# Turning the first FFN's normalised tiles by plain transposes, starting the fifth down product's weight sums in the first, and pairing two late modulation vectors

## The chip, the core and the metric

The kernel runs on one core of one Trainium2 chip. The metric is device time in microseconds (us) of one execution, start to end, on that core. Engines are named as the profile names them: PE is TensorE's matmul stream and PEld its weight loads, DVE is VectorE, ACT is ScalarE, POOL is GpSimd, SP is SyncE. SP starts most of the loads from DRAM (queue q1), POOL starts the accumulating ones (queue q0), ACT a few small ones.

## The reference, cut to what matters

Two layers of a hybrid backbone work on 512 latent and 256 context tokens with D = 1024. Layer 0 has a mixer of gated linear attention and softmax attention, layer 1 a recurrent mixer (HGRN2); after each comes a SwiGLU FFN with 2816 hidden columns. Every sub-layer is wrapped in norms and modulated by vectors m that are computed from the conditioning vector c. Only the latent stream is returned.

```python
def _rms(x, gain): return x * rsqrt(mean(x * x) + 1e-6) * gain
def _modulate(h, shift, scale): return h * (1 + scale) + shift
def _swiglu(h, w_gate, w_up, w_down): return (silu(h @ w_gate) * (h @ w_up)) @ w_down

for l in range(2):
    m = split(silu(c) @ mod_w[l] + mod_b[l], 6)         # for latent tokens; the same with c_ctx for context
    h = _modulate(_rms(x, norm_pre_mix[l]), m[0], m[1])
    o = mixer_l(h)
    x = x + m[2] * _rms(o @ w_out, norm_post_mix[l])
    h = _modulate(_rms(x, norm_pre_ffn[l]), m[3], m[4])
    x = x + m[5] * _rms(_swiglu(h, ...), norm_post_ffn[l])
```

## The kernel before, in words

All data is float32. A matmul of full precision is made of three in the faster fp32r type: each operand is split into a high part H (an ACT cast of the value) and a low part L (DVE: the value less H), and `mm3` adds H·H, H·L and L·H in PSUM. So each weight tile that comes from DRAM as `raw` costs one ACT cast (`wH`) and one DVE subtraction (`wL`) before PE can use it.

Tokens stand in six tiles of 128 (four latent, two context), and the hidden dimension in blocks of 128. A tile has its tokens in the partitions. A matmul wants the hidden dimension there, so a normalised tile has to be turned in eight blocks of 128x128; `h` holds the turned H and L parts.

In order of time, by the profiled execution: the even mixer and its out-projection (to about 420 us), the first FFN's gate and up matrices (about 430 to 749), its down matrix (749 to 911), the odd mixer's first product (to 986) and the rest of that mixer with its out-projection (to about 1345), the second FFN (its down matrix from about 1562 to 1667) and the end.

**The FFN's body.** Gate and up are computed by a Strassen-like scheme of seven products for two halves of the tokens and of the columns, for eleven pairs of column blocks. Between the products `fill` (L1595) takes a step of a generator called `extra`, which is `mod_late` (L560) in the first FFN: it computes the modulation vectors that are needed later. One job of `mod_late` loads the 1024x1024 blocks of `mod_w` in eight row strips, multiplies each by the conditioning value of its rows and adds it to an accumulator `macc` on DVE (L597 and the line of the first strip), one operation for each strip and vector. When all strips are in, eight matmuls with a vector of ones (`mod_acc<-macc,one`) sum the partitions, the sums are turned on PE into columns, and a copy puts them where they are used. `macc` has room for two vectors, and PE's eight matmuls are the same whether one or two of them are in use. `per` says how many DVE operations make a step. A job whose last entry is a tuple also makes gate rows in DRAM (`gate_rows`): one more small turn and a store. The code's steps that are left are taken at the ninth of the eleven pairs (L1665). This part isn't pinned: a planner may shift instructions within an engine's order.

**The down matrix (`down`, L1690).** It is cut into quarters B(k, j), rows k and columns j, and computed by seven products named 11, S1, N3, SN, S3, 22 and 12, each over eleven row blocks in six groups: one block, then five times two. `operands` (L1728) makes a product's weights and factors for one group, two or three groups ahead of PE. It is pinned: the order of the code is kept. Weights come from three places:
- 11, N3 and 12 load a quarter as `raw` on SP's queue.
- S1, SN and 22 use t, a sum that grows: in product 11, t3 is loaded with B(0,1) and DVE writes t = B(0,0) + t3; in S1, POOL's accumulating load adds B(1,1) to t; in SN it adds B(1,0).
- S3 uses t3 + B(1,1): B(0,1) is there since product 11, and POOL's accumulating load adds B(1,1) in product N3 (L1768).

The sums of product 11's first three groups are owed: they are run after `finish()` of the body, the others at once.

**The first FFN's end.** In product 12 each finished tile goes through `post_norm` (the gated residual `xr`), then `pre_norm` (L679): ACT's square with a row sum, a power on POOL (`rs`, L668), which is the factor 1/rms of each token. Here two ways part. At the mixers' ends (`forms`), DVE scales the tile by rs (`xn`, L695) and PE turns xn by transposes with the identity (L358). At the first FFN's end DVE scales the 128x128 identity instead (`dg`, L689), and a matmul of the tile by dg turns and scales in one. `pair_turn` (L715) does this for two tiles at a time: four groups of four 128x128 blocks into one PSUM tile, then for each group two ACT operations that modulate into `hf`, ACT's cast to H and DVE's subtraction to L (L734, L735). The groups are taken one by one between the token tiles of the odd mixer's first product (`nat`), by `turn_step`. From the start of product 12 to the last turned group, `order_from` and `order_to` tie the instructions of ACT and DVE to the order of the code.

Of the kernel before, what the change touches and what calls it, by code (L numbers as in the profile page):

```python
# [8 lines left out]
F32 = mybir.dt.float32  # L9
# [4 lines left out]
ALU = mybir.AluOpType  # L14
# [3 lines left out]
P = 128  # L18
D = 1024
# [11 lines left out]
R_C, R_CC, R_NPM, R_MB, R_NQM, R_NPF, R_NQF, R_BG, R_LB, R_GG, R_HG, R_END = 0, 8, 16, 32, 128, 144, 160, 176, 180, 212, 213, 214  # L31
# [285 lines left out]
class Net:  # L317
# [358 lines left out]
        self.squared = self.nc.scalar.activation(junk, src, AF.Square, accum_out=ss)  # L676
        return ss

    def pre_norm(self, pool, t, xt, A, B, h):  # L679

        nc = self.nc
        r = 0 if t < LT else 1
        forms = isinstance(h, Forms)
        xn = pool.tile([P, D], F32, tag="xn", bufs=2, name=f"xn{t}") if forms else None
        rs = self.rstd(self.sumsq(xt, xn), D)
        yield
        if not forms:
            dg = pool.tile([P, P], F32, tag="dg", bufs=4, name=f"dg{t}")
            self.mark = nc.vector.tensor_scalar(dg, self.ident, rs, None, op0=ALU.mult)  # L689
            self.pair.append((xt, dg))  # L690
            if len(self.pair) == 2:
                self.turns.append(self.pair_turn(pool, t - 1, self.pair, A, B, h))
                self.pair = []
            return
        self.mark = nc.vector.tensor_scalar(xn, xt, rs, None, op0=ALU.mult)  # L695

        def turn():
            for hf in range(2):
                pt = self.tr_tile(f"hT{t}{hf}")
                f = h.at(hf, t)  # L700
                for kk in range(4):
                    k = hf * 4 + kk
                    self.tr(pt[:, kk * P : (kk + 1) * P], xn[:, k * P : (k + 1) * P], self.ident)
                for kk in range(4):
                    k = hf * 4 + kk
                    src = pt[:, kk * P : (kk + 1) * P]
                    nc.scalar.activation(f[:, kk, :], src, AF.Identity, bias=B[:, r, k : k + 1], scale=A[:, r, k : k + 1])
                h.put(hf, t)

        self.turns.append(turn)  # L710

    def pair_turn(self, pool, t, pair, A, B, h):

        nc = self.nc
        r = 0 if t < LT else 1  # L715
        tok = slice(t * P, t * P + 2 * P)

        for q in range(4):
            pt = self.tr_tile(f"hT{t}{q}").rearrange("p (k i) -> p k i", k=2)
            f = pool.tile([P, 2, 2 * P], F32, tag="hf", bufs=2, name=f"hf{t}{q}")  # L720
            for kk in range(2):
                k = 2 * q + kk
                for a, (xt, dg) in enumerate(pair):
                    self.mm(pt[:, kk, a * P : (a + 1) * P], xt[:, k * P : (k + 1) * P], dg, start=True, stop=True)
            for kk in range(2):
                k = 2 * q + kk
                nc.scalar.activation(f[:, kk, :], pt[:, kk, :], AF.Identity, bias=B[:, r, k : k + 1], scale=A[:, r, k : k + 1])
            self.latest = self.put(h, slice(2 * q, 2 * q + 2), tok, f)
            if q < 3:
                yield  # L730
# [777 lines left out]
    def post_pre(self, pp, y, t, gvs, xsrc, xdst, nxt, cuts):  # L1508

        nc = self.nc  # L1510
        xt = pp.tile([P, D], F32, tag="xt", bufs=2 if nxt and isinstance(nxt[2], Forms) else 4, name=f"xr{t}")
        nc.sync.dma_start(out=xt, in_=xsrc(t))

        def store(c):
            nc.sync.dma_start(out=xdst(t)[:, c], in_=xt[:, c])

        yield from self.post_norm(y, xt, gvs[0 if t < LT else 1], cuts, xdst and store)
        if nxt is not None:
            A, B, h = nxt
            yield from self.pre_norm(pp, t, xt, A, B, h)  # L1520

    def turn(self, left=0):

# [182 lines left out]
    def down(self, l, fp, qp, rp, xp, quad, early, tiles, n, ending, finish):  # L1706


        nc = self.nc
        np_, nh = NFC // 2, n // P  # L1710
        B = lambda k, j, i: self.blocks[k][:, i, 512 * j : 512 * j + 512]
        groups = [slice(0, 1)] + [slice(i, i + 2) for i in range(1, 11, 2)]
        ng = len(groups)
        v = nc.vector
# [5 lines left out]
        t, t3 = (lambda i: part(1, i)), (lambda i: part(0, i))  # L1720
        spare = []
        turns = [0, 0]
        add = lambda o, src: self.pin(nc.gpsimd.dma_start(out=o, in_=src, accum_op=ALU.add))  # L1723
        load = lambda o, src: nc.sync.dma_start(out=o, in_=src)
        seven = (("11", "X"), ("S1", "O"), ("N3", "Q"), ("SN", "X"), ("S3", "X"), ("22", "O"), ("12", "X"))
        owed = []

        def operands(p, g):  # L1728
            i = groups[g]
            m = i.stop - i.start  # L1730
            name = seven[p][0]
# [12 lines left out]
            a = [x[:, :m] for x in rings[turns[1] % 3]]  # L1744
            turns[1] += 1
            if name in ("N3", "S3"):
                f = spare[0][:, turns[0] % 2, :m]
                turns[0] += 1
                if name == "N3":
                    v.tensor_tensor(f, quad(0, 0, i), quad(0, 1, i), op=ALU.add)  # L1750
                else:
                    v.scalar_tensor_tensor(f, quad(1, 1, i), -1.0, quad(0, 0, i), op0=ALU.mult, op1=ALU.subtract)
            else:
                f = quad(*{"11": (0, 0), "S1": (1, 0), "SN": (0, 0), "22": (1, 1), "12": (0, 1)}[name], i)
            nc.scalar.copy(H, src)
            nc.scalar.copy(a[0], f)
            v.tensor_tensor(L, src, H.bitcast(F32), op=ALU.subtract)  # L1757
            v.tensor_tensor(a[1], f, a[0].bitcast(F32), op=ALU.subtract)
            if name == "11":
                owed.append(lambda: v.tensor_tensor(t(i), src, t3(i), op=ALU.add))  # L1760
                if g > 2:
                    owed.pop()()
            elif name == "S1":
                x = quad(0, 0, i)
                v.tensor_tensor(x, f, x, op=ALU.subtract)
                add(t(i), B(1, 1, i))
            elif name == "N3":
                add(t3(i), B(1, 1, i))  # L1768
            elif name == "SN":
                add(t(i), B(1, 0, i))  # L1770
            return a, (H, L)
# [12 lines left out]
        dp, y = yield  # L1784
# [81 lines left out]
    def run(self):  # L1866
        nc, I, out = self.nc, self.I, self.out
# [17 lines left out]
        h = Split(ha)  # L1885
        with self.pool("pre0") as pp:
            xT = pp.tile([P, KD, NT], F32, name="xT")
            for t in order:
                xt = pp.tile([P, D], F32, tag="xt", bufs=6, name=f"xt{t}")
                nc.sync.dma_start(out=xt, in_=xin(t))  # L1890
                rs = self.rstd(self.sumsq(xt), D)
                nc.vector.tensor_scalar(xt, xt, rs, None, op0=ALU.mult)
                for hf in range(2):
                    pt = self.tr_tile(f"xT{t}{hf}")
                    for kk in range(4):
                        k = hf * 4 + kk
# [6 lines left out]
            A = self.cst.tile([P, 2, 8], F32, name="aff01")  # L1903
            B = self.mod_m(0, 0)
# [17 lines left out]
            def sums(qd, ks):  # L1922
                if ks[0] == 0:
                    accs[qd] = (self.sc_tile("mod_acc", qd) if qd < 2 else self.tr_tile("mod_acc"))[:, :P]
                for k in ks:
                    for j in range(4):
                        self.mm(
                            accs[qd][32 * j : 32 * j + 32, :],
                            self.scT[:, k, :],
                            us[qd, k // 2 * 2][:, k % 2, j // 2, (j % 2) * P : (j % 2) * P + P],  # L1930
                            start=(k == 0),
                            stop=(k == KD - 1),
                            tile_position=(0, 32 * j),
                        )
                if ks[-1] == KD - 1:
                    accs[qd] = self.mod_cols(0, accs[qd], P, [(m, r, 2 * qd, 2 * m, r, 2) for m in range(2) for r in range(2)])
# [89 lines left out]
        fp = self.open_pool("f0", "right")  # L2026
        mods = self.mod_late(fp, ((1, ((0, 0), (0, 1)), None),), tag="raw", bufs=3)
        forms, pp, rp = project(0, order, yp, I["even_w_out"][0], cat, xin, mods)
        for _ in mods:
            pass  # L2030
        h1 = Split(ha)
        late = self.mod_late(
            fp, ((0, ((5, 0), (5, 1)), (5, R_NQF)), (1, ((1, 0), (1, 1)), None), (1, ((5, 0),), (5, R_NQF, 1)), (1, ((4, 0),), None)),
            per=lambda n: 2 if n > 1 else 3,
        )

        def ending(dp):
# [66 lines left out]
        fp = self.open_pool("f1", "right")  # L2104
# [98 lines left out]
```

## Time and profile before

| | us |
|---|---|
| median of three runs | 1684.37 |
| the three runs | 1682.98, 1684.37, 1687.10 |
| the profiled execution | 1683.48 |
| its span in the trace | 1681.5 |
| PE busy | 1644.6 |
| PEld busy | 1481.0 |
| DVE busy | 1309.8 |
| ACT busy | 917.5 |
| POOL busy | 121.4 |

Times of instructions are counted from the start of the profiled span. The profile has one line for an instruction or a group of them: engine, source line, operation, the output tile and its inputs by name, partitions x elements and type, and the count. "[0.44 <-POOL rs L668]" says that the engine was idle for 0.44 us before it, and that this idle time ended when POOL had written rs. Groups show shortest/mean/longest ns of one instruction and the stretch in which they lie. L355 is the line of the helper through which all matmuls go, L358 that of all transposes, so such instructions are told apart by their tiles.

### The profile page before, as it was taken

Reading aid. Unit: us, or ns where it says so; the run is one execution under the profiler, and the core shown is the slowest. Engines: PE = TensorE matmul, PEld = TensorE weight load, DVE = VectorE, ACT = ScalarE, POOL = GpSimd, SP = SyncE. Lnnn points to the kernel's source line nnn. Section 1 sums busy time; section 2 is a strip of 40 time slices with the busy share of each in tenths; the row PEclk is TensorE's granted clock in tenths of the full one; section 3 lists DMA queues with packets and bytes.
Section 4 is the critical chain, followed back from the end, with each engine's and each line's share of the span. In section 5 each row is a group of like instructions: output and inputs, shape, how many; then the busy total and the mean of one; then the engine's idle time right before and its main releaser. Section 6 shows DMA issues by size and latency. Waiting matters only on the chain.

```text
span 1681.5 us, 32537 instructions
## 1 busy us (share of the span) xinstructions
PE 1644.6 (98%) x13407; PEld 1481.0 (88%) x13407; DVE 1309.8 (78%) x2105; ACT 917.5 (55%) x1560; POOL 121.4 (7%) x129
## 2 busy tenths in 40 slices
PE   6999998999999999999999999999999999999998
PEld 5899997888999999998888888888888899999876
DVE  4889768876898988877668548788775599987887
ACT  4745567836543443445447436666664565555654
POOL 1004110001000000003102000000000100000220
PEclk9999999999999999999999999999999999999999
DMA  9651002164243444348725542121124334333793
GB/s 330 192 155 41 2 27 101 51 207 152 84 147 101 144 143 148 117 150 167 142 73 203 190 129 59 51 64 39 52 64 150 125 111 117 113 101 101 183 206 138
DMA packets 184736, 204.79 MB, mean 122 GB/s; under 512 B 7142, under 2 KB 141836, under 8 KB 184588
## 3 DMA queue, kind: packets, MB, share of 16 engines
q1 hardware_dynamic: 173632, 181.82, 34.3%
q0 software_dynamic: 9024, 17.30, 5.9%
q10 hardware_dynamic: 1932, 3.59, 0.7%
q8 instruction: 105, 1.72, 0.4%
q14 instruction: 43, 0.35, 0.1%
HBM read 193.23 MB, written 9.46 MB: 121 GB/s over the span
## 4 chain that ended last, share of the span: by engine, by line
PE 85%; DVE 7%; ACT 3%; DMA 3%; issue 1%; POOL 0%; ACTq 0%; DVEq 0%; POOLq 0%
PE nat L355 13%; PE a L355 12%; PE ff L355 8%; PE E L355 8%; PE x L355 7%; PE oproj L355 6%; PE o L355 4%; PE D L355 4%; PE b L355 4%; PE fq L355 3%; PE gqk L355 2%; PE pearly L355 2%; PE S L355 2%; PE poh L355 1%; PE attO L355 1%
## 5 line engine op out<-in xcount | busy, mean ns | idle before, releaser
L355 PE MATMUL nat<-wH,x 128*128 128x256 f32 (+2 forms) x968 | 225.5, 321 | 3.0 <-ACT x L734 2.6
L355 PEld LDWEIGHTS nat<-wH,x 128*128 128x128 f32 x968 | 162.2, 190 | 19.2 <-ACT x L734 3.7
L824 ACT CAST wH<-raw 128x1024 fp32r<-128x1024 f32 x120 | 125.0, 1050 | 95.5 <-DVE raw L849 31.4
L825 DVE TENSOR_TENSOR wL<-raw,wH 128x1024 fp32r<-128x1024 f32 x120 | 145.6, 1220 | 21.3 <-ACT wH L824 20.9
L355 PE MATMUL nat<-wL,x 128*128 128x256 f32 (+2 forms) x484 | 153.4, 317 | 0.3 <-DVE wL L770 0.3
L770 DVE TENSOR_TENSOR wL<-raw,wH 128x1024 fp32r<-128x1024 f32 (+1 forms) x83 | 98.7, 1198 | 48.0 <-ACT wH L769 47.1
L355 PE MATMUL ff<-x,wH 128*128 128x512 f32 (+1 forms) x512 | 127.7, 340 | 0.0
L769 ACT CAST wH<-raw 128x1024 fp32r<-128x1024 f32 (+1 forms) x83 | 84.9, 1034 | 68.0 <-PE ff L355 19.9
L668 POOL TENSOR_TENSOR rs<-ms,neghalf 128x1 f32<-128x1 f32 (+2 forms) x62 | 63.5, 1029 | 783.0 <-DVE ms L666 782.9
L355 PE MATMUL oproj<-wH,x 128*128 128x512 f32 x320 | 102.1, 396 | 0.4 <-ACT x L1290 0.4
L355 PEld LDWEIGHTS nat<-wL,x 128*128 128x128 f32 x484 | 92.1, 190 | 6.0 <-DVE wL L770 0.7
L597 DVE SCALAR_TENSOR_TENSOR macc<-mraw,scT,macc 128x1024 f32<-128x1024 f32 x70 | 88.1, 1280 | 10.9 <-DMA mraw<-in_mod_w_dram 10.7
L355 PEld LDWEIGHTS ff<-x,wH 128*128 128x128 f32 x512 | 87.2, 190 | 10.1
L355 PE MATMUL x<-wH,two 128*128 128x512 f32 x280 | 90.5, 392 | 0.9 <-DVE y L1798 0.7
L976 ACT COPY qkh<-arr 128x512 f32<-128x512 f32 x112 | 70.2, 643 | 36.3 <-DVE arr L981 32.1
L1723 POOL DMA_DIRECT2D t<-in_ffn_w_down_dram x36 | 41.8, 1228 | 648.1 <-DVE wL L1757 613.5
L355 PE MATMUL ff<-x,wL 128*128 128x256 f32 (+1 forms) x256 | 86.2, 337 | 0.0
L849 DVE TENSOR_TENSOR raw<-raw 128x512 f32<-128x512 f32 x120 | 82.7, 690 | 2.8
L981 DVE TENSOR_TENSOR arr<-arr,f 128x512 f32<-128x512 f32 x112 | 74.2, 687 | 1.9 <-ACT qkh L976 0.3
L355 PE MATMUL E<-x,wH 128*128 128x384 f32 (+1 forms) x320 | 70.9, 311 | 0.0
L355 PEld LDWEIGHTS oproj<-wH,x 128*128 128x128 f32 x320 | 59.5, 188 | 12.6 <-ACT x L1290 0.9
L355 PE MATMUL b<-x,wH 128*128 128x384 f32 (+1 forms) x320 | 70.5, 309 | 0.0
(420 smaller groups left out, 4540.7 us busy)
## 6 DMA issues: line engine op xcount, KB each, us to landing
mraw<-in_mod_w_dram SPq DMA_DIRECT2D x80, 512.0 KB, 4.4
raw<-in_ffn_w_gate_dram SPq DMA_DIRECT2D x44, 512.0 KB, 4.6
raw<-in_ffn_w_up_dram SPq DMA_DIRECT2D x44, 512.0 KB, 4.3
raw<-in_odd_w_in_dram SPq DMA_DIRECT2D x40, 512.0 KB, 3.8
t<-in_ffn_w_down_dram POOLq DMA_DIRECT2D x30, 512.0 KB, 8.0
raw<-in_ffn_w_down_dram SPq DMA_DIRECT2D x28, 512.0 KB, 7.4
mraw<-in_mod_w_dram SPq DMA_DIRECT2D x32, 256.0 KB, 6.3
raw<-in_even_w_in_dram SPq DMA_DIRECT2D x16, 512.0 KB, 3.8
```

Of the source, the lines that this page charges most:

```text
L355: return self.pin(self.nc.tensor.matmul(*a, **k))
L597: nc.vector.scalar_tensor_tensor(a, u, w, a, op0=ALU.mult, op1=ALU.add)
L668: nc.gpsimd.tensor_tensor(rs, ms, self.neghalf.to_broadcast([P, w]), op=ALU.pow)
L769: nc.scalar.copy(H[:, :m], raw[:, :m])
L770: nc.vector.tensor_tensor(L[:, :m], raw[:, :m], H[:, :m].bitcast(F32), op=ALU.subtract)
L824: self.nc.scalar.copy(H, f)
L825: self.nc.vector.tensor_tensor(L, f, H.bitcast(F32), op=ALU.subtract)
L849: add = lambda o, x, y: nc.vector.tensor_tensor(o, x, y, op=ALU.add)
L976: nc.scalar.copy(qkv[:, :, :, half, :], dst)
L981: nc.vector.tensor_tensor(dst, dst, tb, op=ALU.mult)
L1723: add = lambda o, src: self.pin(nc.gpsimd.dma_start(out=o, in_=src, accum_op=ALU.add))
```

## The change

Three edits, independent of each other.

The first makes the first FFN's end like the mixers' ends: DVE scales the whole tile into xn, which takes the place of the tile y (no longer read then), and PE turns it by transposes with the identity.

```diff
-    def pre_norm(self, pool, t, xt, A, B, h):
+    def pre_norm(self, pool, t, xt, A, B, h, xn):
...
-            dg = pool.tile([P, P], F32, tag="dg", bufs=4, name=f"dg{t}")
-            self.mark = nc.vector.tensor_scalar(dg, self.ident, rs, None, op0=ALU.mult)
-            self.pair.append((xt, dg))
+            self.mark = nc.vector.tensor_scalar(xn, xt, rs, None, op0=ALU.mult)
+            self.pair.append(xn)
...
-                for a, (xt, dg) in enumerate(pair):
-                    self.mm(pt[:, kk, a * P : (a + 1) * P], xt[:, k * P : (k + 1) * P], dg, start=True, stop=True)
+                for a, xn in enumerate(pair):
+                    self.tr(pt[:, kk, a * P : (a + 1) * P], xn[:, k * P : (k + 1) * P], self.ident)
...
-            yield from self.pre_norm(pp, t, xt, A, B, h)
+            yield from self.pre_norm(pp, t, xt, A, B, h, y)
```

The second moves the accumulating loads of t3, in both FFNs, from the third product to the first, each right behind its group's sum t.

```diff
             if name == "11":
-                owed.append(lambda: v.tensor_tensor(t(i), src, t3(i), op=ALU.add))
+
+                def sums():
+                    v.tensor_tensor(t(i), src, t3(i), op=ALU.add)
+                    add(t3(i), B(1, 1, i))
+
+                owed.append(sums)
                 if g > 2:
                     owed.pop()()
...
-            elif name == "N3":
-                add(t3(i), B(1, 1, i))
```

The third makes the last two jobs of `mod_late` in the first FFN, of one vector each (the second layer's 5 and 4), one job of two. The gate rows then come after the pair, and a step is always two DVE operations.

```diff
-            fp, ((0, ((5, 0), (5, 1)), (5, R_NQF)), (1, ((1, 0), (1, 1)), None), (1, ((5, 0),), (5, R_NQF, 1)), (1, ((4, 0),), None)),
-            per=lambda n: 2 if n > 1 else 3,
+            fp, ((0, ((5, 0), (5, 1)), (5, R_NQF)), (1, ((1, 0), (1, 1)), None), (1, ((4, 0), (5, 0)), (5, R_NQF, 1))),
+            per=lambda n: 2,
```

More of the change, by code (lines that the diff above doesn't have):

```diff
@@ L683, in pre_norm @@
         forms = isinstance(h, Forms)
-        xn = pool.tile([P, D], F32, tag="xn", bufs=2, name=f"xn{t}") if forms else None
-        rs = self.rstd(self.sumsq(xt, xn), D)
+        if forms:
+            xn = pool.tile([P, D], F32, tag="xn", bufs=2, name=f"xn{t}")
+        rs = self.rstd(self.sumsq(xt, xn if forms else None), D)
         yield
         if not forms:
-            dg = pool.tile([P, P], F32, tag="dg", bufs=4, name=f"dg{t}")
-            self.mark = nc.vector.tensor_scalar(dg, self.ident, rs, None, op0=ALU.mult)
-            self.pair.append((xt, dg))
+            self.mark = nc.vector.tensor_scalar(xn, xt, rs, None, op0=ALU.mult)
+            self.pair.append(xn)
             if len(self.pair) == 2:
```

## Prediction

> **What bounds the kernel now.** I read the page first, then the list of waits, then the timeline of each stage that the change touches.
>
> ```profile
> span 1681.5 us, 32537 instructions
> PE 1644.6 (98%) x13407; PEld 1481.0 (88%) x13407; DVE 1309.8 (78%) x2105; ACT 917.5 (55%) x1560; POOL 121.4 (7%) x129
> ```
>
> TensorE (PE) is busy 98% of the span, so an instruction less on PE is worth its issue time, unless PE then waits for another engine. That has to be read stage by stage. The windows give the body of the first FFN and its end: us, then busy us (and records) of PE, its weight loads, DVE, ACT and POOL, granted clock, DMA share, GB/s.
>
> ```profile
> 430.00:740.00 310.00, 310.00 (x1804) 305.34 (x1802) 270.09 (x346) 137.29 (x198) 0.00 (x0) 1.00 0.39 118
> 895.00:945.00 50.00, 49.21 (x264) 41.93 (x263) 30.78 (x48) 36.41 (x64) 6.65 (x11) 1.00 0.43 147
> ```
>
> In the body PE has no idle time at all (310.00 of 310.00). In the end it is idle for 0.8 us of 50, and ACT is busy for 36 of 50 where the body has 137 of 310: there ACT and DVE may be close behind PE. That decides the first part.
>
> **The change part by part: the tiles' turning.** Today DVE scales the identity (dg) and a matmul by dg turns and scales at once; then DVE scales the whole tile (xn) and PE only transposes. The parts have rows: dg and its products here, xn and its transposes from the mixers' ends, which are made that way already.
>
> ```profile
> L355 PE MATMUL hT<-dg,xr x96: 270/275/377, 901.7 to 941.2; 128*128 128x128 f32 x96
> L689 DVE TENSOR_SCALAR dg<-ident,rs x6: 278/284/289, 895.5 to 929.2; 128x128 f32<-128x128 f32 x6
> L358 PE MATMUL hT<-ident,xn x80: 270/273/330, 378.3 to 1345.7; 128*128 128x128 f32 x80
> L695 DVE TENSOR_SCALAR xn<-xr,rs x10: 743/754/755, 372.0 to 1342.8; 128x1024 f32<-128x1024 f32 x10
> 904.76 1.05 PE L355 MATMUL hT<-dg,xr 128*128 128x128 f32 x8
> 905.57 0.48 PE L355 MATMUL x<-wH,two 128*128 128x512 f32 x1
> ...
> 381.14 0.66 PE L358 MATMUL hT<-ident,xn 128*128 128x128 f32 x4
> 381.55 0.70 PE L355 MATMUL oproj<-wH,x 128*128 128x512 f32 x2
> ```
>
> Six tiles of eight blocks are 48 products but 96 records: a product with dg runs as two instructions. Ten xn tiles are 80 transposes and 80 records. A group of four products holds PE for 905.57 - 904.76 = 0.81 us, four transposes for 381.55 - 381.14 = 0.41. Twelve groups save 12 x 0.40 = 4.8 us of PE, the bound if nothing else is late. DVE pays 0.754 - 0.284 = 0.47 us more for each of six tiles.
>
> Between the seventh product's start and the last turned tile ACT and DVE keep the order of the code (order_from, order_to), so the delays can be carried down the rows.
>
> ```profile
> 902.27 0.28 DVE L689 TENSOR_SCALAR dg<-ident,rs 128x128 f32<-128x128 f32 x1
> 903.23 1.06 ACT L676 ACTIVATE junk<-y 128x1024 bf16<-128x1024 f32 x1 [2.14 <-DVE y L1798]
> ...
> 916.36 0.50 PE L355 MATMUL nat<-wL,x 128*128 128x512 f32 x1 [0.31 <-DVE wL L770]
> ...
> 918.83 0.29 DVE L689 TENSOR_SCALAR dg<-ident,rs 128x128 f32<-128x128 f32 x1 [0.67 <-POOL rs L668]
> 920.66 1.06 ACT L676 ACTIVATE junk<-xr 128x1024 bf16<-128x1024 f32 x1 [1.80 <-DVE xr L755]
> 930.13 0.69 DVE L735 TENSOR_TENSOR x<-hf,x 128x512 fp32r<-128x512 f32 x1 [0.68 <-ACT x L734]
> ...
> 936.42 0.69 DVE L735 TENSOR_TENSOR x<-hf,x 128x512 fp32r<-128x512 f32 x1 [5.59 <-ACT x L734]
> ```
>
> First pair: two scalings stand ahead of the DVE sum y that starts ACT at 903.23, and ACT's next idle time begins only at 920.66 - 1.80 = 918.86. So ACT starts 2 x 0.47 = 0.94 us later. The third scaling adds 0.47, of which short waits of DVE swallow about 0.36, and the wL for which PE waits at 916.36 already (0.31) comes 1.05 later; so the 1.6 us that its first four groups saved are waited away: PE stands at +1.05 at 916.36. Second pair: the scaling at 918.83 lies just ahead of its group, so PE stands at +1.4; four groups bring back 1.6, but the second group after waits about 0.2 for its PSUM buffer, which ACT frees. The last half tile at 930.13 comes 1.2 later; its end, 930.82, lies some half microsecond ahead of its use, so PE is pushed back to +0.7. Third pair: DVE waits 5.59 us there, nothing is close, and 1.6 come off. **Sum: -0.9 us** of the 4.8; the other bound, with no gain from the transposes at all and the delays kept, is +1.4.
>
> What could make it less is POOL's power for the next tile, which runs beside DVE.
>
> ```profile
> 907.33 0.55 POOL L668 TENSOR_TENSOR rs<-ms,neghalf 128x1 f32<-128x1 f32 x1 [5.78 <-DVE ms L666]
> 910.08 1.39 POOL L668 TENSOR_TENSOR rs<-ms,neghalf 128x1 f32<-128x1 f32 x1 [2.21 <-DVE ms L666]
> 909.85 1.22 DVE L770 TENSOR_TENSOR wL<-raw,wH 128x1024 fp32r<-128x1024 f32 x1
> ```
>
> The same power takes 0.55 us alone and 1.39 beside a wide DVE operation. Two powers follow right on a scaling that grows longer (918.83 and 922.73); if both are stretched by 0.84, up to 1.7 us are lost. I take nothing, since the powers start before the scaling, and keep it for the range. The Trainium skill (SBUF — State Buffer, "SBUF: two separate sides") says that VectorE and GpSimd share a port pair as an exclusive lock, which a VectorE operation in a two-port mode holds for its whole length. The two POOL rows agree; by that rule the part would give +0.8 in place of -0.9.
>
> **The pair of late vectors.** Two jobs of one vector become one job of two.
>
> ```profile
> 685.48 0.34 PE L355 MATMUL D<-x,wL 128*128 128x384 f32 x1
> 685.75 1.06 PE L355 MATMUL mod_acc<-macc,one 128*32 128x512 f32 x8
> 686.75 0.62 PE L355 MATMUL E<-x,wH 128*128 128x384 f32 x2
> ```
>
> A job's end is one group of eight ones-records and four transposes of the summed rows. A record of the body holds PE for 310.00 / 1804 = 0.17 us, so D's last ends its hold at 685.65 and the ones-records hold PE until 686.75: 1.1 us. Four transposes hold it for 0.41 by the row at 381.14. One such end goes: **-1.5 us**, whole, because PE has no idle time here. The sixteen weight loads and multiply-adds stay; eleven steps stay eleven (two vectors' sums in eight steps instead of twice three, one end instead of two). The drain at the ninth pair now holds a gate row instead of a column; its transpose is only moved. Bounds: -1.7, if the record behind each group is late as well, and 0, if PE turns out to wait instead.
>
> **The fifth product's sums.** POOL's six accumulating loads of t3 leave the third product and follow the sums of the first, in both FFNs. POOL's queue keeps its order, so they stand ahead of the second product's loads of t. The question is who else uses DMA then. Here are packets and MB, first of the SP queue (q1) alone at 749 to 757, then of POOL's (q0) and SP's together at 1598 to 1606; then what ACT and PE wait for.
>
> ```profile
> q1 hardware_dynamic: 1335, 2.57, 92.9%
> ...
> q0 software_dynamic: 541, 1.03, 69.8%
> q1 hardware_dynamic: 537, 1.02, 38.8%
> ...
> 753.97 1.06 ACT L1755 CAST wH<-raw 128x1024 fp32r<-128x1024 f32 x1 [1.38 <-DMA raw<-in_ffn_w_down_dram]
> 764.48 0.62 PE L355 MATMUL x<-wH,two 128*128 128x512 f32 x2
> 1602.00 1.05 ACT L1755 CAST wH<-raw 128x1024 fp32r<-128x1024 f32 x1 [4.01 <-DMA raw<-in_ffn_w_down_dram]
> ...
> PEld q L355 <- ACT aH L1756: 0.6, 1, 0.6
> PEld q L355 <- DVE wL L1757: 0.6, 1, 0.6
> ```
>
> Alone, SP's loads run at 0.32 MB a us; beside POOL's they share packet for packet and run at 0.13. In the first FFN the first product's last three raw loads are still to come when t3's first sums are ready (from about 751), and ACT waits for them even now (753.97). At the shared rate I put their arrivals at 757, 761 and 763 instead of 754, 755 and 757. The tightest use is the fifth group's low part at 764.48, for which raw at 761, its cast of 1.06 and DVE's two subtractions (1.22 for the weight's, by the wL row above, and about as much for the factor's) end at 764.5. So I take **+0.3 us**, bounds 0 and +2.5. In the second FFN the raws of the first product are there long before; the third product's late loads (ACT's 4.01 us wait) meet POOL's queue as before, since the second product's sums, moved back by t3's, now fill it until about 1606. So no gain there either; the bounds are PE's two longest waits in that product, the last two rows (from the list of waits between 1556 and 1670): -1.2 if they go, and as much again, +1.2, if one more sum stands ahead of those loads. POOL's issues hide behind PE; t3 is wanted only two products after its old place.
>
> **Sum:** -0.9 - 1.5 + 0.3 = -2.1 us. The profiled execution took 1683.5 us (span 1681.5 and 2.0 around it), so **1681.4 us**; that execution lies 0.9 under the median of before, 1684.4.
>
> **The rivals.** *All PE time arrives.* If ACT and DVE have more slack than the rows say, the turning gives 4.8: 1683.5 - 4.8 - 1.5 = 1677.2 us. For it: PE is idle there for 0.8 us in all. Against it: ACT's 15.6 us without idle time, and the wait at 916.36. *POOL's loads go first.* If the first products' loads must stand behind all queued sums instead of sharing, the third raw load of the first FFN arrives near 760 and costs PE 2.5 us; the third product of the second FFN loses 1.2 more. With the stretched powers (1.7) that is -2.1 + 2.5 - 0.3 + 1.2 + 1.7 = +3.0: 1686.5 us, slower. It decides from the point where the fourth group's raw lands after about 758.5. Against it: 541 and 537 packets side by side. *The turning stays two-pass or the planner reorders the unpinned stretches* so that the pair's end is not saved: about 1683.5, no change.
>
> **How the numbers follow.** Forecast 0.50, all PE time 0.22, loads behind sums 0.18, no change 0.10. The range 1677.0 to 1687.0 reaches to the first rival's time and to the slower one's. A measurement of this kernel tells about 0.3%, 5 us, from no change. Faster than that are most of the first rival (0.18) and the forecast where the second FFN's stall goes too (0.04): 0.22. Slower than that is only the slower rival with its stalls in both FFNs at more than my price: 0.10. The rest, 0.68, is within.
>
> **What would show it.** hT must fall from 96 records to 48 in the end, its groups from 0.81 to 0.4 us; PE's waits for DVE or ACT between 903 and 932 must grow to about 3 us. If they do not, the first step is wrong. The ones-records must fall by eight with no new idle time in the body. In the first FFN's first product ACT must wait longer for raw, and PE little or not; a PE wait there of 2 us says the slower rival. In the second FFN the third product's wait for raw must stay near 4 us; if it goes, its stall of some 1.2 us is gain that I left out.

## The result, and the profile after

The changed kernel takes 1681.69 us (median of 20 runs, 1680.08 to 1683.9) where the kernel before takes 1684.32 (20 runs, 1682.5 to 1687.1): 2.6 us less, a ratio of 0.9985 with a 95% interval of 0.9979 to 0.9991. The forecast was 1681.4. The sum was right, but two of its terms were not, and by luck they cancelled.

The profiled execution took 1680.08 us. The head of its page, and the windows of the first FFN's body and of its end with the same columns as before:

```profile
span 1678.3 us, 32400 instructions
PE 1638.8 (98%) x13347; PEld 1474.3 (88%) x13347; DVE 1312.2 (78%) x2104; ACT 916.9 (55%) x1560; POOL 122.6 (7%) x129
```

```profile
430.00:740.00 310.00, 309.34 (x1794) 305.15 (x1793) 269.48 (x345) 137.01 (x198) 0.00 (x0) 1.00 0.40 118
895.00:945.00 50.00, 46.31 (x219) 35.80 (x218) 34.19 (x49) 36.35 (x64) 7.89 (x11) 1.00 0.44 147
```

PE is busy for 1644.6 - 1638.8 = 5.8 us less, but the span is shorter by 3.2 only: more than two microseconds of the time saved on PE came back as idle time. The windows say where. At the first FFN's end PE is now idle for 3.7 us of 50 (0.8 before), and in the body, where it never stood still, for 0.66.

To place the gains, the start of the same matmul is compared in the two traces. A shift is the start after less the start before; where it changes, time went or came.

| matmul that starts, in the trace of before, at | shift, us | what lies between it and the row above |
|---|---|---|
| 600, first FFN's body | +0.48 | the start of the run; no edit lies here |
| 700, first FFN's body | 0.00 | the pair of late vectors: -0.48 |
| 891, before the last tiles of the down matrix | +0.04 | t3's sums in the first FFN: 0 |
| 916.36, the nat that waits for wL | +1.07 | first pair of tiles: +1.03 |
| 922, behind the second pair's first group | +0.70 | |
| 931.6, after the second pair | +1.02 | second pair: about 0 |
| 941.2, after the third pair | -0.69 | third pair: -1.71 |
| 1371, second FFN's start | -0.39 | no edit lies here |
| 1412, second FFN's body | -1.45 | no edit lies here |
| 1604, third product of its down matrix | -1.47 | |
| 1610, fourth product | -3.07 | t3's sums in the second FFN, if anything: -1.60 |

The first FFN's end, by the list of PE's waits from 895 to 945 in the changed kernel, and the rows of its timeline in which these waits end:

```profile
PE nat L355 <- DVE wL L770: 1.8, 2, 1.3
PE hT L358 <- DVE y L689: 1.6, 2, 1.2
PE hT L358 <- ACT hf L727: 0.2, 1, 0.2
```

```profile
903.57 0.55 PE L358 MATMUL hT<-ident,y 128*128 128x128 f32 x3 [1.21 <-DVE y L689]
914.50 0.50 PE L355 MATMUL nat<-wL,x 128*128 128x512 f32 x1 [0.56 <-DVE wL L770]
917.44 0.50 PE L355 MATMUL nat<-wL,x 128*128 128x512 f32 x1 [1.27 <-DVE wL L770]
920.72 0.55 PE L358 MATMUL hT<-ident,y 128*128 128x128 f32 x3 [0.37 <-DVE y L689]
```

The nat at 917.44 is the one that started at 916.36 before. hT has 48 records of one pass where it had 96, and PE pays for it with 3.6 us of waits for the scaled tile and for the wL that stands behind the scalings on DVE.

The body's new idle time is one place. PE first, then DVE, from the changed kernel's timeline:

```profile
676.39 0.59 PE L355 MATMUL E<-T,wH 128*128 128x384 f32 x2 [0.20 <-DVE go L902]
677.43 0.44 PE L355 MATMUL E<-T,wL 128*128 128x384 f32 x1 [0.46 <-DVE wL L825]
```

```profile
669.76 1.28 DVE L597 SCALAR_TENSOR_TENSOR macc<-mraw,scT,macc 128x1024 f32<-128x1024 f32 x1
672.44 1.29 DVE L597 SCALAR_TENSOR_TENSOR macc<-mraw,scT,macc 128x1024 f32<-128x1024 f32 x1 [1.39 <-DMA mraw<-in_mod_w_dram]
673.64 2.13 DVE L849 TENSOR_TENSOR raw<-raw 128x512 f32<-128x512 f32 x3
675.70 0.55 DVE L902 TENSOR_TENSOR go<-go,E 128x384 f32<-128x384 f32 x1
676.16 1.22 DVE L825 TENSOR_TENSOR wL<-raw,wH 128x1024 fp32r<-128x1024 f32 x1
```

Read from below: PE waits for go and wL; DVE makes them late because it stood still for 1.39 us at 672.44, for a load of mod_w that the second vector of the pair needs in the same step. The two waits are 0.66 us in the rows; -0.48 is left of the 1.5 us that one group of sums less should save, so with what they stretch around them they cost about 1.0 us.

The first product of the first FFN, whose loads now share DMA with t3's sums (the changed kernel's timeline of ACT):

```profile
754.68 1.05 ACT L1755 CAST wH<-raw 128x1024 fp32r<-128x1024 f32 x1 [2.09 <-DMA raw<-in_ffn_w_down_dram]
758.45 1.05 ACT L1755 CAST wH<-raw 128x1024 fp32r<-128x1024 f32 x1 [2.71 <-DMA raw<-in_ffn_w_down_dram]
762.49 1.05 ACT L1755 CAST wH<-raw 128x1024 fp32r<-128x1024 f32 x1 [2.26 <-DMA raw<-in_ffn_w_down_dram]
```

ACT waits longer there, as forecast, and PE doesn't notice: the shift stays at 0.04.

In the second FFN the third product's stall is gone. DMA by queue from 1602 to 1610 (packets, MB, time as a share of 16 engines), in the kernel before and then in the changed one:

```profile
q0 software_dynamic: 543, 1.05, 70.5%
q1 hardware_dynamic: 545, 1.04, 39.2%
```

```profile
q1 hardware_dynamic: 904, 1.72, 57.8%
q0 software_dynamic: 292, 0.53, 39.3%
```

POOL's queue (q0) moves half as much there, and SP's loads (q1) two thirds more. That is not yet why the stall is gone: the load on which it hangs had landed by then, as the last experiment shows.

### The profile page after: what moved, and what is told of

Same layout as the page of the kernel before. It is cut to its first block, busy times and chain, and to the rows that moved or that the text cites. A ratio compares the mean times of both kernels' runs of the same rounds, so it can differ in the third digit from the quotient of the medians.

```text
span 1678.3 us, 32400 instructions
## 1 busy us (share of the span) xinstructions
PE 1638.8 (98%) x13347; PEld 1474.3 (88%) x13347; DVE 1312.2 (78%) x2104; ACT 916.9 (55%) x1560; POOL 122.6 (7%) x129
## 4 chain that ended last, share of the span: by engine, by line
PE 84%; DVE 7%; ACT 4%; DMA 2%; issue 2%; POOL 1%; DVEq 0%; ACTq 0%; POOLq 0%
PE nat L355 12%; PE a L355 11%; PE ff L355 8%; PE E L355 8%; PE x L355 6%; PE oproj L355 6%; PE o L355 4%; PE b L355 4%; PE D L355 4%; PE pearly L355 3%; PE fq L355 3%; PE gqk L355 2%; PE q L355 2%; PE S L355 2%; PE poh L355 1%
```

## The experiments

All times are medians, of 11 runs (20 for the changed kernel); the ratio is to runs of the kernel before on the same chip. The shifts are read from the profiles as above, as changes over a stage: the body (600 to 700; 500 to 700 in the two spaced kernels), the first FFN's end (891 to 941), the second FFN's start (1371 to 1412), its third product (1604 to 1610). The stall of that product is 1.6 us long in the first profile of the kernel before, so -1.60 in the last column says that it is gone, and 0 that it is all there.

| kernel | us | ratio and interval | body | FFN's end | second FFN's start | third product |
|---|---|---|---|---|---|---|
| changed | 1681.69 | 0.9985 [0.9979, 0.9991] | -0.48 | -0.73 | -1.06 | -1.60 |
| before_again | 1683.97 | 0.9997 [0.9988, 1.0005] | +0.37 | +0.01 | -0.15 | -0.11 |
| turn_only | 1683.50 | 0.9996 [0.9987, 1.0005] | +0.23 | -0.74 | -0.08 | -1.59 |
| sums_only | 1682.90 | 0.9992 [0.9984, 1.0001] | +0.01 | 0.00 | +0.69 | -1.59 |
| pair_only | 1684.51 | 1.0002 [0.9994, 1.0011] | +0.30 | 0.00 | +2.59 | -0.07 |
| third_pair | 1681.34 | 0.9985 [0.9976, 0.9994] | -0.16 | -1.77 | +0.06 | -1.59 |
| short_tr | 1682.03 | 0.9992 [0.9983, 1.0000] | +0.50 | -2.14 | -0.79 | -1.16 |
| long_mm | 1684.42 | 1.0005 [0.9996, 1.0014] | +0.02 | +1.50 | -0.38 | -0.72 |
| pair_oneload | 1681.60 | 0.9987 [0.9979, 0.9996] | -1.65 | 0.00 | +0.02 | -1.60 |
| pair_second | 1682.98 | 1.0000 [0.9991, 1.0009] | -0.20 | +0.01 | -0.68 | -1.59 |
| pair_spaced | 1684.13 | 0.9997 [0.9988, 1.0006] | -0.12 | +0.04 | -0.09 | -1.60 |
| third_spaced | 1681.34 | 0.9984 [0.9976, 0.9993] | -0.10 | -1.50 | +0.40 | -1.59 |
| sums_later | 1685.99 | 1.0011 [1.0002, 1.0019] | +0.66 | +0.04 | -0.35 | -1.60 |

What an edit leaves alone shows how much the run itself moves. The first FFN's end moves by no more than 0.04 where the first edit is absent, so 0.1 us can be read there. The body without the third edit lies between 0.00 and +0.66 against the first profile. The second FFN's start moves between -1.06 and +2.59, whatever the edit. In pair_only, where it moves by +2.59, the granted clock is 0.89 from 1371 to 1386, where every other profile has 1.00; so at least a part of that figure is the clock's.

### The kernel before once more

No edit.

> The kernel before once more, for what the run alone moves: the start (up to 1.9 us between the profiles so far), the second FFN's start between 1370 and 1412 (from 1.1 us earlier to 2.6 later), the stall of 1605 to 1609 (there or not). If the stall is there again: it belongs to the place of t3's sums. If not: it comes by the run in the kernel before, and the second edit takes away only a chance of it.

The stall of the third product is there again: 1.5 of the 1.6 us. The body moves by +0.37 without any edit. The changed kernel's 1.06 us at the second FFN's start are put down to the run and not to the edits: before_again has -0.15 there, and the three edits alone have -0.08, +0.69 and +2.59. None of them shows a gain there; that the three together make one isn't excluded.

### Each edit alone

The first edit alone:

```diff
-            self.mark = nc.vector.tensor_scalar(dg, self.ident, rs, None, op0=ALU.mult)
+            self.mark = nc.vector.tensor_scalar(xn, xt, rs, None, op0=ALU.mult)
...
-                    self.mm(pt[:, kk, a * P : (a + 1) * P], xt[:, k * P : (k + 1) * P], dg, start=True, stop=True)
+                    self.tr(pt[:, kk, a * P : (a + 1) * P], xn[:, k * P : (k + 1) * P], self.ident)
```

> The kernel before with the first edit alone. Theory of the carried delays (the two longer scalings stand ahead of ACT and DVE work that PE waits for): the same matmuls after the first FFN's end start 0.7 us earlier than before, with PE 1.0 us later than before near 916, hT's waits on DVE grown, and the rest of the run unmoved; in all -0.7 us. Rival (the turning brings all its 4.8 us of PE time, and the changed kernel lost the rest elsewhere): -4 us or more at 941.

-0.74 us at 941, with the same waits as in the changed kernel, and the rival's -4 is nowhere. But the third product's stall went too, which this edit does not touch.

The second edit alone:

```diff
+                    add(t3(i), B(1, 1, i))
...
-            elif name == "N3":
-                add(t3(i), B(1, 1, i))
```

> The kernel before with the second edit alone. Theory (POOL's queue, empty between the first and the second product of the second FFN, now works there, so its sums are done before the third product's loads need the bandwidth): the stall at 1605 to 1609 goes, -1.5 us there and 0 in the first FFN; in all -1.5 us. Rival (that stall went because PE and DVE came to it in another phase, from the other two edits): no gain there, 0 us.

-1.59 us at the third product and 0 in the first FFN, as the theory had it. Beside turn_only this alone proves nothing: there the stall was gone without the edit.

The third edit alone:

```diff
-(1, ((5, 0),), (5, R_NQF, 1)), (1, ((4, 0),), None)),
-            per=lambda n: 2 if n > 1 else 3,
+(1, ((4, 0), (5, 0)), (5, R_NQF, 1))),
+            per=lambda n: 2,
```

> The kernel before with the third edit alone. Theory (one end's 1.5 us go, but DVE waits 1.4 us for mod_w's load just ahead of a product whose sum PE wants, and PE loses 1.0 us near 676): -0.5 us by the end of the first FFN's body. Rival (the stall near 676 came from the run and not from the edit): -1.5 us. The second FFN's start, which came 1.1 us earlier in the changed kernel between 1370 and 1412, is untouched by this edit; if it moves here too, it moves by itself.

PE's waits in the body, from the list of waits from 500 to 745 of this kernel:

```profile
PE E L355 <- DVE go L902: 0.6, 1, 0.6
PE E L355 <- DVE wL L825: 0.5, 1, 0.5
```

The same stall, so it belongs to the edit. The body moved by +0.30, no better than kernels without the edit (0.00 to +0.66).

In its total none of the three edits alone can be told from the kernel before: each interval holds 1. Their medians differ from that of the kernel before on their chip (1683.87) by -0.37, -0.97 and +0.64 us, -0.7 together, where the changed kernel has -2.6; intervals of some 1.5 us either way allow both. So the prices of the edits rest on the stages, and not on the totals.

### The turning: which half costs what

Two kernels cross the prices of PE and DVE. In short_tr DVE still makes the short dg, and PE turns the unscaled tile by transposes:

```diff
-                    self.mm(pt[:, kk, a * P : (a + 1) * P], xt[:, k * P : (k + 1) * P], dg, start=True, stop=True)
+                    self.tr(pt[:, kk, a * P : (a + 1) * P], xt[:, k * P : (k + 1) * P], self.ident)
```

> The kernel before with DVE's short scaling (dg) kept and PE's products by dg replaced by plain transposes of the unscaled tile. It leaves the scaling by 1/rms out of the first FFN's end, so that PE has the price of after and DVE that of before. Theory of the carried delays: without them the first pair's gain is still waited away at 916 (that wL was waited for before), the second pair keeps a part and the third all: -2 to -3 us at 941. Rival (only DVE's scaling holds PE back): -4.8 us.

In long_mm DVE scales the whole tile, and PE keeps its two-pass matmul, by the plain identity (the lines are against the first edit):

```diff
-                    self.tr(pt[:, kk, a * P : (a + 1) * P], xn[:, k * P : (k + 1) * P], self.ident)
+                    self.mm(pt[:, kk, a * P : (a + 1) * P], xn[:, k * P : (k + 1) * P], self.ident, start=True, stop=True)
```

> The kernel before with DVE's long scaling (xn) and PE's matmuls kept, now by the plain identity: PE has the price of before and DVE that of after. Theory of the carried delays: PE is late by 1.0 us at 916 and ends the stage at +1.1 to +1.5 us. Rival (DVE's longer scaling is hidden while PE has its old length): 0 us.

The four corners, by the shift over the stage: short scaling and matmuls 0.00 (before), long scaling and matmuls +1.50, short scaling and transposes -2.14, long scaling and transposes -0.74. They add up: the longer scaling costs 1.4 to 1.5 us with either kind of product, and the transposes bring 2.1 to 2.2 of their 4.8 with either kind of scaling. So even a free scaling would leave more than half of PE's saving behind. The list of PE's waits from 895 to 945 in short_tr names what holds it:

```profile
PE nat L355 <- DVE wL L770: 2.0, 3, 1.2
PE hT L358 <- ACT hf L727: 0.5, 1, 0.5
```

These are the weights' low parts on DVE and the turned tile's way through ACT, and they do not depend on how a tile is scaled. (Of the 2.14 us 1.3 are lost again between 941 and 981 in that kernel. The eight records of the next late vectors' sums come there as two groups of four, the second waits for DVE's macc, and from the first to the next product's start it is 2.30 us, from 978.21 to 980.51, where the kernel before has 0.99, from 979.50 to 980.49.)

### The third pair alone

The changed kernel, with the first two pairs by dg as before:

```diff
+            self.normed += 1
+            if self.normed > 4:
+                self.mark = nc.vector.tensor_scalar(xn, xt, rs, None, op0=ALU.mult)
+                self.pair.append((xn, None))
+            else:
+                dg = pool.tile([P, P], F32, tag="dg", bufs=4, name=f"dg{t}")
...
+                    if dg is None:
+                        self.tr(o, i, self.ident)
+                    else:
+                        self.mm(o, i, dg, start=True, stop=True)
```

> The changed kernel, but with the first edit for the third pair of tiles alone; the first two pairs are scaled and turned by dg as before. Theory of the carried delays: the first two pairs cost more by DVE's longer scaling than they bring, the third brings all its 1.6 us, so PE stands at -1.6 at 941 against the kernel before (beside what the other edits moved) where the changed kernel stood at -0.7: 0.9 us better than the changed kernel. Rival (each pair brings its share of what the edit brings): a third of 0.7, so 0.5 us worse than the changed kernel.

The list of PE's waits from 895 to 945 is that of the kernel before:

```profile
PE hT L355 <- DVE dg L695: 0.5, 1, 0.5
PE nat L355 <- DVE wL L780: 0.3, 1, 0.3
```

-1.77 us where the whole edit brings -0.73: a third of the transposes brings more than twice what all of them bring. The two groups of hT in this kernel stand side by side, 64 records for 32 products by dg and 16 records for 16 transposes (busy time, mean ns): 0.27 us busy for a product and 0.15 for a transpose.

```profile
L355 PE MATMUL hT<-dg,xr 128*128 128x128 f32 x64 | 8.7, 277 | 0.5 <-DVE dg L695 0.5
L358 PE MATMUL hT<-ident,y 128*128 128x128 f32 x16 | 2.4, 272 | 0.0
```

The whole kernel's median, 1681.34, can't be told from the changed kernel's: the 1.0 us are seen in the stage, not in the total.

### The pair of vectors: load or work

In pair_oneload both vectors of the pair use one load for each row strip, eight loads less, while DVE's work stays.

```diff
-            steps = [(k, m) for k in range(KD) for m in sorted({m for m, _ in ms})]
+            shared = l == 1 and ms == ((4, 0), (5, 0))
+            steps = [(k, m) for k in range(KD) for m in sorted({m for m, _ in ms})][:: 2 if shared else 1]
...
-                    if mm != m:
+                    if mm != m and not shared:
```

> The kernel before with the third edit, where the pair's two vectors share one load of mod_w for each row strip. It computes the second layer's vector 5 from the columns of vector 4, so half of the pair's loads are left out and DVE's work stays. Theory (DVE waits for the pair's second load): the stall near 676 goes, -1.5 us by 731. Rival (DVE's work, closer to PE by the 1.1 us gained before, makes it): -0.5 us as with the edit alone.

-1.65 us in the body, no wait of PE, no wait of DVE for mod_w. So the load is what costs, and DVE's work has room. In pair_second the pair comes ahead of the job for vector 1 (the lines are against the third edit):

```diff
-(1, ((1, 0), (1, 1)), None), (1, ((4, 0), (5, 0)), (5, R_NQF, 1))
+(1, ((4, 0), (5, 0)), (5, R_NQF, 1)), (1, ((1, 0), (1, 1)), None)
```

> The kernel before with the third edit and the pair put ahead of the job that computes the second layer's vector 1 for both streams, which needs one load for two multiply-adds. The last steps before 676 then wait for no second load. Theory: no stall near 676; if the pair's loads are covered in their new place, -1.5 us by 731. Rival (the pair meets the same wait in its new place, 544 to 592): -0.5 us, with the stall there.

The rival had it: the stall moves with the pair. DVE and then PE in that kernel's timeline:

```profile
597.39 1.28 DVE L597 SCALAR_TENSOR_TENSOR macc<-mraw,scT,macc 128x1024 f32<-128x1024 f32 x1 [2.21 <-DMA mraw<-in_mod_w_dram]
```

```profile
603.56 0.59 PE L355 MATMUL E<-T,wH 128*128 128x384 f32 x2 [0.83 <-DVE qa L902]
```

In pair_spaced the pair's steps are single multiply-adds, and a third step in each product of seven makes room for them:

```diff
             elif wn == "U2":
                 nc.scalar.copy(c12, pt)
+                if self.third is not None:
+                    self.third()
...
+            self.third = fill if not l and 4 <= idx <= 8 else None
...
-            per=lambda n: 2 if n > 1 else 3,
+            per=lambda n: 2 if n < 2 else 1,
```

> The kernel before with the third edit, and from the fourth of the body's pairs of column blocks on a third step in each product of seven, where a step of the vector pair is one multiply-add instead of two, so that each of its loads has a step's time to land. Theory (the price is DVE's wait for the second load of a step): no PE wait in the body, -1.5 us by 731 against the same run's place at 600. Rival (DVE has no room for the pair's work near PE's use): the stall comes back in another place, -0.5 us or less.

Half right. PE has no wait in the body, so the spacing covers the load. But the body moved by -0.12 only. The planner, free to shift instructions there, cut the sums of another job in two:

```profile
582.72 1.05 PE L355 MATMUL mod_acc<-macc,one 128*32 128x512 f32 x4
583.70 0.62 PE L355 MATMUL E<-x,wH 128*128 128x384 f32 x2
584.25 1.05 PE L355 MATMUL mod_acc<-macc,one 128*32 128x512 f32 x4
585.23 0.44 PE L355 MATMUL E<-x,wL 128*128 128x384 f32 x1
```

Each half holds PE from its start to the next product's for 0.98 us, as long as the whole group of eight did (1.0 from 685.75 to 686.75 before). So 0.98 of the 1.5 us saved on one job's end was spent here; the rest lies within what the body moves without the edit (0.00 to +0.66). A version that keeps these eight records together wasn't tried.

Both better forms together:

> The changed kernel with the first edit for the third pair of tiles alone and the pair of vectors spaced as in pair_spaced. Theory: the two better forms add up, 1.0 us for each against the changed kernel: 2 us under it, some 4.5 us under the kernel before. Rival (the runs' own spread at the start and in the second FFN's start covers it): no less than the changed kernel.

A miss: 1681.34 us, the same as third_pair. The sums are cut in two here as in pair_spaced (581.04 and 582.57). It and third_pair have the lowest medians of the study, but neither is clear of the changed kernel's.

### t3's sums the other way

```diff
-            elif name == "N3":
-                add(t3(i), B(1, 1, i))
             elif name == "SN":
+                add(t3(i), B(1, 1, i))
                 add(t(i), B(1, 0, i))
```

> The kernel before with t3's accumulating loads moved the other way, from the third product to the fourth. Theory (t3's sums share the bandwidth with the third product's own loads, and it is these that stall PE at 1605 to 1609): the stall of the second FFN's third product goes as it does in the changed kernel, up to -1.6 us. Rival (the second product's sums of t make it): the stall stays, up to 1.6 us by the run. A stall was there in four of the seven profiles with t3's sums in the third product and in none of the three with them in the first.

DMA from 1602 to 1610 in this kernel:

```profile
q1 hardware_dynamic: 1035, 1.99, 74.8%
q0 software_dynamic: 18, 0.02, 1.6%
```

With t3's sums out of the third product the loads have the queue to themselves and the stall is gone (-1.60). The time is lost again later: the fourth product has twelve sums to wait for, the shift grows by 1.1 us between 1610 and 1649, and the kernel is slower than before (1.0011, interval from 1.0002).

Counted over all profiles, the stall is there in five of the nine with t3's sums in the third product (1.6, 1.5, 1.5, 0.9 and 0.4 us, 0.7 as a mean over the nine) and in none of the five with them earlier or later. So these sums alone don't make it: in turn_only, pair_oneload, pair_second and pair_spaced they stand where they stood, and it is gone.

What it hangs on can be read from one instruction, ACT's cast of the third product's last raw load. Here it is in the kernel before, in turn_only (sums in the old place, no stall) and in the changed kernel:

```profile
1606.04 1.05 ACT L1755 CAST wH<-raw 128x1024 fp32r<-128x1024 f32 x1 [2.47 <-DMA raw<-in_ffn_w_down_dram]
```

```profile
1604.37 1.05 ACT L1755 CAST wH<-raw 128x1024 fp32r<-128x1024 f32 x1 [2.87 <-DMA raw<-in_ffn_w_down_dram]
```

```profile
1602.22 1.05 ACT L1755 CAST wH<-raw 128x1024 fp32r<-128x1024 f32 x1 [2.44 <-PE q L355]
```

Less each profile's shift at 1604 this cast starts at 1606.04, 1605.98, 1605.94, 1605.33 and 1604.90 in the five with the stall, and between 1603.1 and 1604.35 in the nine without. The stall is, within 0.02 us, what the cast is later than 1604.45. So it is there when that load lands too late for PE, and the limit is close on both sides. SP's loads ran at different rates on the way. In the 12 us of PE's work that are 1592 to 1604 in the kernel before (1592.8 to 1604.8, 1590.5 to 1602.5 and 1593.6 to 1605.6 in the others' own time) they moved 1.02 MB there, 1.24 in turn_only, 1.22 in the changed kernel and 1.81 in sums_later.

That t3's sums delay this load is shown by sums_later: its cast starts at 1603.1 on the same scale. How much the second edit is worth isn't shown: five stalls in nine profiles against none in four can be chance, and what lets the load land in time in four of the nine stays open.

## Why the prediction was right, and where it was not

**The turning: right, by its mechanism.** Forecast -0.9, measured -0.73 and -0.74 in two kernels. The carried delays came out nearly row by row: PE at +1.05 at 916.36 (measured +1.07), late again at about +1 after the second pair (+0.7 forecast, +1.02), all of the third pair's 1.6 us (1.71). The waits of PE, forecast at about 3 us, sum to 3.6. The bound for no gain of the transposes, +1.4, was +1.50 in long_mm. The rival that all PE time arrives failed on what spoke against it, the wL at 916.36. The stretch of POOL's powers came, but small. The same two rows of POOL in the changed kernel and in short_tr, which lacks the long scaling:

```profile
911.06 1.69 POOL L668 TENSOR_TENSOR rs<-ms,neghalf 128x1 f32<-128x1 f32 x1 [2.21 <-DVE ms L666]
919.32 1.37 POOL L668 TENSOR_TENSOR rs<-ms,neghalf 128x1 f32<-128x1 f32 x2 [6.58 <-DVE ms L666]
```

```profile
910.90 1.40 POOL L668 TENSOR_TENSOR rs<-ms,neghalf 128x1 f32<-128x1 f32 x1 [2.20 <-DVE ms L666]
918.98 1.06 POOL L668 TENSOR_TENSOR rs<-ms,neghalf 128x1 f32<-128x1 f32 x2 [6.68 <-DVE ms L666]
```

0.3 us each, not 0.84; the power of 922.14 in the kernel before, the other one that the prediction named, also takes 0.3 more (1.37 at 923.53, 1.06 in short_tr). That agrees with the sense of the rule that the prediction took from the Trainium skill (SBUF — State Buffer, "SBUF: two separate sides"), but the +0.8 that was worked out from it did not come.

**The pair of vectors: the failed step is "whole, because PE has no idle time here".** The saving of 1.5 us is real (-1.65 where the second load is left out). But an engine without idle time isn't one with nothing close behind it. DVE was busy for 270 of 310 us there, and its macc waited for mod_w already. The page of the kernel before has 10.7 us of such waits in the whole run (busy time and mean ns, then idle time before and what ended most of it):

```profile
L597 DVE SCALAR_TENSOR_TENSOR macc<-mraw,scT,macc 128x1024 f32<-128x1024 f32 x70 | 88.1, 1280 | 10.9 <-DMA mraw<-in_mod_w_dram 10.7
```

The text costed the sixteen loads as staying, without asking how they follow each other. Two multiply-adds in one step need two loads of which only one is ahead; DVE waits 1.4 us for the second just before it makes go and wL, and PE runs into that. The wait as such is not new. Before, a step of these two jobs had three multiply-adds and three loads, and DVE waited for mod_w in the body for 3.7 us in seven waits (the longest 1.06) where the changed kernel has 2.5 in four (the longest 1.39); no wait of PE came of the 3.7. What differs is that one long wait now lies right ahead of what PE uses next. The prediction had named 0 as a bound "if PE turns out to wait instead". It took the other end.

**t3's sums in the first FFN: right.** Loads later by 0.7 to 5 us, of which PE saw 0.04; forecast 0.3. The arrivals were forecast at 757, 761 and 763, and ACT's casts started at 754.7, 758.5 and 762.5, all somewhat sooner.

**t3's sums in the second FFN: the failed step is that the third product's late loads "meet POOL's queue as before" and that there is "no gain there either".** The first half of the reasoning came true. The second product's sums were moved back: the last of them landed at 1605.33 in the changed kernel and at 1600.45 in the kernel before, and from 1605.4 to 1606 only SP's queue moved anything. The forecast had POOL's queue full "until about 1606". POOL's queue had been nearly empty ahead of them, so that t3's sums found some room. DMA from 1566 to 1582, before and after:

```profile
q0 software_dynamic: 42, 0.09, 5.6%
```

```profile
q0 software_dynamic: 1065, 2.05, 69.7%
```

All six of t3's sums (five of 512 KB and one of 256) were issued between 1564 and 1580, and 2.05 MB were moved in these 16 us. What failed is the step from a full queue to a load that is late as before. With POOL's queue still at work, the load on which the stall hangs landed at 1602.14. Less the shift of -1.47 that is 1603.6, where it was 1605.96 before, and its cast may start at 1604.45 without making PE wait. The prediction had not set the landing against the time at which PE needs it, and it took the stall for a fixed part of the kernel, which four of nine profiles don't have. It priced the stall at 1.2 by two of PE's waits; it was 1.6.

That packets are taken in turn from both queues was right, and the rule in the Trainium skill (DMA: Bandwidth & Descriptors, "Queues, rings and completion order": each DMA engine goes round its queues packet by packet) agrees with 543 and 545 packets.

**The sum.** The forecast -2.1 was -0.9 - 1.5 + 0.3. Stage by stage the two profiles give -0.7 for the turning, -0.5 for the pair and -1.6 for the third product, beside +0.5 and -1.1 that the run moved. The gain that the pair did not bring (1.0) was made up by the stall that the forecast had left standing: that is luck, the more so as the profiled run of before had the stall whole, where the mean over the nine profiles is 0.7. Had only one of the two gone as said, the total would have missed by more than a microsecond, still inside the range.

## What to carry to other kernels

When PE is saturated, a shorter PE instruction is worth only what the next engine has in hand there: carry the delay of every added DVE operation down the rows to the next PE wait, tile by tile, and make the exchange only where the row behind it shows slack (here the third pair, with its 5.6 us). When two steps are merged, look at the loads as well as at the work: count how many must land within one step and how many buffers are ahead, and see what PE waits for right behind the last of them. And before counting a stall, or counting it out, set the landing of the load that makes it against the time at which it is needed, in more than one profile of the same kernel: a margin of a few tenths of a microsecond can go either way.

## What the runs showed of the chip

Four matmuls of 32 columns each, side by side in the array, two records for each, hold PE for 1.0 us (685.75 to 686.75), and four of the eight records alone hold it for 0.98, as pair_spaced shows. So cutting the group in two doubles its price. A two-pass matmul by a scaled identity holds PE for twice as long as a plain transpose of the same block (0.81 and 0.41 us for four) in float32.
